# Ten staged batches in place of eleven in a sliding-window copy, and one split of the direct copies

## The chip, the core and the metric

The kernel runs on one core of one Trainium2 chip. The metric is device time in microseconds (us); lower is better. The time before is a median of three runs. The profile is of one execution. MB and GB/s are powers of ten; KB in the table of DMA issues are of 1024 bytes.

## The reference

Overlapping windows of 64 rows are copied out of a sequence, one every 32 rows. Nothing is computed; the output is the input written almost twice.

```python
def setup_inputs():
    batch, length, dim = (32, 4096, 256)
    window_size = 64
    stride = 32
    ...
def reference(x, window_size, stride):
    n_windows = (length - window_size) // stride + 1      # 127
    for i in range(n_windows):
        start = i * stride
        result[:, i] = x[:, start:start + window_size].copy()
```

In float32, x is 134.2 MB and the result 266.3 MB.

## The kernel before

A *block* is 32 rows of x, 32 KB. A batch has 128 blocks. Window w of a batch is blocks w and w + 1, so it is 64 KB, and a batch has 127 windows. Inner blocks stand in two windows each. The kernel only issues DMAs. It treats a batch in one of two ways.

*Staged batches* (`staged`, line 143) are 1, 4, 7, ..., 31: eleven of them. A staged batch is loaded once into a tile in SBUF, one block to each of the 128 partitions (4.19 MB), and stored twice from there, once as first halves of windows and once as second halves (8.39 MB). Its engine traffic is 12.58 MB. The stores write 128 half windows each, one more than the batch has, so a staged batch also writes wrong data into a half window of a neighbour. The neighbour's window there is written again later. The last batch, 31, is taken one block earlier so that nothing is written past the end of the output.

*Direct batches* (`direct`, line 146) are the other twenty-one. They are copied from DRAM to DRAM: windows overlap in the read and not in the write, so a window costs 64 KB read and 64 KB written, but passes the DMA engines once.

Three queues issue the work. All their transfers run on the core's same 16 DMA engines.

- ACT's queue (`ring_s`) carries the staged batches. `Staging.run` (line 116) works with six tiles: loads of the first six batches, their stores, loads of the other five, their stores. A load into a used tile waits until the tile's stores have landed (line 90); a store waits for its load (line 100). The first load is cut in four. The last batch's stores are cut as well (lines 103 to 106): the parts that matter for SP's last DMA come first, and five smaller ones (`end`) come last and are counted apart.
- SP's queue (`ring_d`) carries the direct batches: for each, 112 windows in seven *sixteens* of 16 windows (lines 161 to 164). They begin at window 15 where the batch before is staged, otherwise at window 0. Lines 170 to 187 keep an account, `share`, and with it send some sixteens as two *halves*, one DMA for the 16 first halves and one for the 16 second halves. In stretches which the account counts as loads three in four are halved, in others about one in seven (0.15), and all of them at the very start and around the turn to the second loads. Of 147 sixteens 55 are halved (110 DMAs), 92 are whole.
- POOL's queue (`ring_r`) carries the *edges* (line 166): the 15 windows of each direct batch that remain, which include those that a staged neighbour overwrites. POOL waits for `near` (line 192), which is the second last sixteen on SP; then each edge waits for the stores of its staged neighbours (lines 194 to 196). The last direct batch, 30, has its 15 windows in three parts: 4 windows, 9 windows cut into 16 columns (`columns`, line 200), and 2 windows that SP writes when the last staged batch's stores have landed (line 202).

[...]

A packet, in the profile's words, is one piece that a DMA engine moves for a queue. Pieces of loads and stores are cut at 16384 elements (`IN`, `OUT`), those of direct copies at 32768 (`DIRECT`); the packets that the page counts are 16 KB on ACT's queue and 32 KB on SP's. Each DMA adds on each engine it uses one small packet that reports its completion.

Of the kernel before, what the change touches and what calls it, by code (L numbers as in the profile page):

```python
# [125 lines left out]
@with_exitstack  # L126
def kernel(
    ctx: ExitStack,
    tc: tile.TileContext,
    x: bass.AP,  # L130
    window_size: bass.AP,
    stride: bass.AP,
    out: bass.AP,
):
    nc = tc.nc
    W, S = int(window_size), int(stride)
    B, L, D = x.shape
    n_win = (L - W) // S + 1
    assert out.shape == (B, n_win, W, D)
    c = Copier(x, out, B, L, D, W, S, n_win)  # L140


    staged = [*range(1, B, 3)]
    items = [(b, -1 if b == B - 1 else 0, c.nb) for b in staged]
    place = {b: g for g, (b, _, n) in enumerate(items) if n == c.nb}
    direct = [b for b in range(B) if b not in staged]
    pool = ctx.enter_context(tc.tile_pool(name="xb", bufs=1))
    st = Staging(c, tc, pool, x.dtype, items, 6)
    ring_d, ring_s, ring_r = nc.sync, nc.scalar, nc.gpsimd
    done = tc.alloc_semaphore("done")  # L150
    near = tc.alloc_semaphore("near")
    rest = tc.alloc_semaphore("rest")
    total = {done: 0, near: 0, rest: 0}

    def count(dma, sem):
        dma.then_inc(sem, 16)
        total[sem] += 16

    sixteens = []
    for b in direct:
        w = 15 if b - 1 in staged else 0
        sixteens += [(b, w + 16 * j) for j in range((c.nw - w) // 16)]
    singles = [(B - 1, c.nw - 1, 1)]
    edges = [(b, 0 if b - 1 in staged else 112, 15) for b in direct[:-1]]
    last = B - 2
    edges.append((last, 112, 4))

    first_loads, loads, stores = 6 * 17, 5 * 17, 6 * 34  # L170
    turns = share = 0
    with tc.tile_critical():  # L172
        st.run(ring_s)

        for i, (b, w) in enumerate(sixteens):
            sem = near if i == len(sixteens) - 2 else done
            second = turns - first_loads - stores
            loading = turns < first_loads or 0 <= second < loads
            share += 120 if turns < 16 or -8 <= second < 16 else 90 if loading else 18
            if share >= 120:  # L180
                share -= 120
                turns += 4
                count(c.windows(ring_d, b, w, 16, 0), done)
                count(c.windows(ring_d, b, w, 16, 1), sem)
            else:
                turns += 3
                count(c.windows(ring_d, b, w, 16), sem)
            if i == len(sixteens) // 2:
                for b, w, half in singles:
                    count(c.windows(ring_d, b, w, 1, half, 2048), done)  # L190

        ring_r.wait_ge(near, 16)
        for b, w, n in edges:
            for k in (b - 1, b + 1):
                if k in place and b != last:
                    st.wait_stored(ring_r, place[k])
            count(c.windows(ring_r, b, w, n), rest)


        count(c.columns(ring_r, last, 116, 9), rest)  # L200
        ring_r.drain()  # L201
        st.wait_stored(ring_d, place[B - 1])
        count(c.columns(ring_d, last, 125, 2), done)
        total[st.ended] = st.count[st.ended]
        for sem, n in total.items():
            ring_d.wait_ge(sem, n)
# [35 lines left out]
```

## Time and profile before

| | |
|---|---|
| median of 3 runs | 752.55 us (751.88 to 753.92) |
| span of the profiled execution | 742.1 us |
| median less that span | 10.45 us |
| busy time of POOL, the only engine with any | 12.7 us |
| bytes moved by the DMA engines, and mean rate | 313.26 MB, 422 GB/s |
| wait of SP for the last staged batch's stores (line 44) | 169.3 us, until its DMA at 723.77 us |

The profiled execution has no total of its own in the page beside its span; the median of the runs stands 10.45 us above the span.

The page's line of DMA rates shows forty slices of the span, 18.6 us each:

```profile
GB/s 361 424 430 427 435 431 428 423 435 425 428 427 426 428 428 420 429 435 427 427 427 412 433 435 431 427 436 432 434 424 429 430 424 426 428 435 432 421 420 253
```

Only the first and the last slice stand apart. The page's DMA issues show what the queues carry, with the median time from issue to landing in the last column:

```profile
out_dram<-in_x_dram SPq DMA_DIRECT2D x92, 1024.0 KB, 99.8
out_dram<-xb ACTq DMA_DIRECT2D x21, 4096.0 KB, 138.5
out_dram<-in_x_dram SPq DMA_DIRECT2D x110, 512.0 KB, 90.2
xb<-in_x_dram ACTq DMA_DIRECT2D x10, 4096.0 KB, 130.5
out_dram<-in_x_dram POOLq DMA_DIRECT2D x20, 960.0 KB, 37.9
```

A DMA lands some 100 us after its issue: the queues are filled far ahead of the engines. The chain of waits that ended last is of little use here, since 92% of it is put down to "another core or an unknown queue", which are the transfers themselves. So the case is read from the DMA tables, cut by time.

### The profile page before, as it was taken

Reading aid. Unit: us, or ns where it says so; the run is one execution under the profiler, and the core shown is the slowest. Engines: PE = TensorE matmul, PEld = TensorE weight load, DVE = VectorE, ACT = ScalarE, POOL = GpSimd, SP = SyncE. Lnnn points to the kernel's source line nnn. Section 1 sums busy time; section 2 is a strip of 40 time slices with the busy share of each in tenths; the row PEclk is TensorE's granted clock in tenths of the full one; section 3 lists DMA queues with packets and bytes.
Section 4 is the critical chain, followed back from the end, with each engine's and each line's share of the span. In section 5 each row is a group of like instructions: output and inputs, shape, how many; then the busy total and the mean of one; then the engine's idle time right before and its main releaser. Section 6 shows DMA issues by size and latency. Waiting matters only on the chain.

```text
span 742.1 us, 323 instructions
## 1 busy us (share of the span) xinstructions
POOL 12.7 (2%) x26
## 2 busy tenths in 40 slices
POOL 0000000000000000000000000000000000050100
DMA  8999999999999999999999999999999999999996
GB/s 361 424 430 427 435 431 428 423 435 425 428 427 426 428 428 420 429 435 427 427 427 412 433 435 431 427 436 432 434 424 429 430 424 426 428 435 432 421 420 253
DMA packets 18290, 313.26 MB, mean 422 GB/s; under 512 B 4336, under 2 KB 4336, under 8 KB 4528
## 3 DMA queue, kind: packets, MB, share of 16 engines
q1 hardware_dynamic: 8016, 154.32, 48.8%
q10 hardware_dynamic: 9104, 138.41, 44.0%
q0 software_dynamic: 1168, 20.51, 6.6%
q14 instruction: 2, 0.02, 0.0%
HBM read 220.95 MB, written 267.09 MB: 658 GB/s over the span
## 4 chain that ended last, share of the span: by engine, by line
another core or an unknown queue 92%; POOL 2%; issue 0%; POOLq 0%; SPq 0%
POOL out_dram L34 2%; POOLq L201 0%; POOLq L237 0%; SPq L172 0%; POOLq L114 0%
## 5 line engine op out<-in xcount | busy, mean ns | idle before, releaser
L34 POOL DMA_DIRECT2D out_dram<-in_x_dram x21 | 12.0, 575 | 685.4 <-DMA out_dram<-in_x_dram 648.7
L44 POOL DMA_DIRECT2D out_dram<-in_x_dram x1 | 0.6, 581 | 0.0
L223 POOL MEMSET const-float32-0.0<- 128x1 f32 x1 | 0.1, 98 | 0.2 <-issue 0.2
L223 POOL MEMSET const-bfloat16-1.0<- 128x1 bf16 x1 | 0.1, 101 | 0.0
L223 POOL MEMSET const-float32-1.0<- 128x1 f32 x1 | 0.1, 98 | 0.0
L223 POOL MEMSET const-uint8-127<- 128x1 uint8 x1 | 0.1, 98 | 0.0
## 6 DMA issues: line engine op xcount, KB each, us to landing
out_dram<-in_x_dram SPq DMA_DIRECT2D x92, 1024.0 KB, 99.8
out_dram<-xb ACTq DMA_DIRECT2D x21, 4096.0 KB, 138.5
out_dram<-in_x_dram SPq DMA_DIRECT2D x110, 512.0 KB, 90.2
xb<-in_x_dram ACTq DMA_DIRECT2D x10, 4096.0 KB, 130.5
out_dram<-in_x_dram POOLq DMA_DIRECT2D x20, 960.0 KB, 37.9
xb<-in_x_dram ACTq DMA_DIRECT2D x4, 1024.0 KB, 15.7
out_dram<-xb ACTq DMA_DIRECT2D x2, 1024.0 KB, 110.5
out_dram<-xb ACTq DMA_DIRECT2D x4, 512.0 KB, 94.4
```

The lines of the kernel that those rows point to most:

```text
L34: return q.dma_start(out=self.oap((b * self.nw + w0) * 2 + h, [[2 * blk, n], row]), in_=self.xap(b * self.nb + w0 + h, [[blk, n], row]), m ...
L44: return q.dma_start(out=self.oap((b * self.nw + w0) * 2, [[part, 16], [2 * self.blk, n], row]), in_=self.xap(b * self.nb + w0, [[part, 16 ...
L223: nc = _bacc.Bacc("TRN2", target_bir_lowering=False, num_devices=1)
```

## The change

Batch 25 leaves the staged list and becomes direct, so ten batches are staged: six and four. Twenty-two are direct. The account is gone, and no sixteen is halved: each direct batch is sent as 16, 16, 16, 32, 16 and 16 windows, at all times. `near` is still the second last piece. [...]

```diff
-    staged = [*range(1, B, 3)]
+    staged = [1, 4, 7, 10, 13, 16, 19, 22, 28, B - 1]
...
-    sixteens = []
+    pieces = []
     for b in direct:
         w = 15 if b - 1 in staged else 0
-        sixteens += [(b, w + 16 * j) for j in range((c.nw - w) // 16)]
+        for n in (16, 16, 16, 32, 16, 16):
+            pieces.append((b, w, n))
+            w += n
...
-    edges.append((last, 112, 4))
-
-    first_loads, loads, stores = 6 * 17, 5 * 17, 6 * 34
-    turns = share = 0
+    odd = -15 * len(edges) % 16
+    edges.append((last, 112, odd))
...
-        for i, (b, w) in enumerate(sixteens):
-            sem = near if i == len(sixteens) - 2 else done
-            second = turns - first_loads - stores
-            loading = turns < first_loads or 0 <= second < loads
-            share += 120 if turns < 16 or -8 <= second < 16 else 90 if loading else 18
-            if share >= 120:
-                share -= 120
-                turns += 4
-                count(c.windows(ring_d, b, w, 16, 0), done)
-                count(c.windows(ring_d, b, w, 16, 1), sem)
-            else:
-                turns += 3
-                count(c.windows(ring_d, b, w, 16), sem)
-            if i == len(sixteens) // 2:
+        for i, (b, w, n) in enumerate(pieces):
+            count(c.windows(ring_d, b, w, n), near if i == len(pieces) - 2 else done)
+            if i == len(pieces) // 2:
                 for b, w, half in singles:
                     count(c.windows(ring_d, b, w, 1, half, 2048), done)
...
-        count(c.columns(ring_r, last, 116, 9), rest)
+        count(c.columns(ring_r, last, 112 + odd, 13 - odd), rest)
```

## The prediction

> **What bounds the kernel now.** I read the page's share of busy time first. It shows no engine but POOL, at 12.7 us in all, so the span is made of transfers. The second view is the page's table of DMA queues:
>
> ```profile
> span 742.1 us, 323 instructions
> ...
> DMA packets 18290, 313.26 MB, mean 422 GB/s; under 512 B 4336, under 2 KB 4336, under 8 KB 4528
> ...
> q1 hardware_dynamic: 8016, 154.32, 48.8%
> q10 hardware_dynamic: 9104, 138.41, 44.0%
> q0 software_dynamic: 1168, 20.51, 6.6%
> ...
> HBM read 220.95 MB, written 267.09 MB: 658 GB/s over the span
> ```
>
> q1 is SP's queue (direct copies, DRAM to DRAM), q10 is ACT's (staged loads and stores), q0 is POOL's (edges). The shares add to 99.4% of 16 engines' span: the DMA engines are full, and a byte taken off them should shorten the span. One row stands against that at once: a direct byte is read and written in HBM, so it counts there twice and a staged byte once, and HBM already moves 658 GB/s.
>
> The third view was the DMA table cut into stretches, because the loads and stores of the staged batches alternate. From the byte counts, the first six loads end near 130 us, their stores near 405, the next five loads near 505, and the last stores at the end. Here are, one after the other, stretches 20 to 120 (loads), 140 to 400 (stores), 420 to 500 (loads) and 520 to 640 us (stores):
>
> ```profile
> DMA packets 2607, 42.86 MB, mean 429 GB/s; under 512 B 685, under 2 KB 685, under 8 KB 685
> q1 hardware_dynamic: 1299, 22.74, 53.1%
> ...
> DMA packets 6176, 111.19 MB, mean 428 GB/s; under 512 B 1312, under 2 KB 1312, under 8 KB 1328
> q1 hardware_dynamic: 3088, 63.48, 57.4%
> ...
> DMA packets 2109, 34.56 MB, mean 432 GB/s; under 512 B 560, under 2 KB 560, under 8 KB 560
> q1 hardware_dynamic: 1056, 18.35, 53.4%
> ...
> DMA packets 2838, 51.47 MB, mean 429 GB/s; under 512 B 597, under 2 KB 597, under 8 KB 597
> q1 hardware_dynamic: 1418, 29.53, 57.7%
> ```
>
> The rate is nearly the same in all four, 428 to 432. q1's part of the bytes is 53.1% in both load stretches (22.74 of 42.86; 18.35 of 34.56) and 57.1 to 57.4% in the store stretches. In the long store stretch both queues have 3088 packets: they take turns, packet by packet. The sizes follow: 16 KB on ACT's queue (138.41 MB over 9104 less one completion packet per DMA and engine), 32 KB on SP's. A full sixteen gives each engine three turns (two of 32 KB, one completion), a pair of halves four. With three quarters of the sixteens halved, that is 65.5/3.75 = 17.5 KB a turn against ACT's 16.4 x 16/17 = 15.4: 53.1%, the measured load stretch. With 15% halved, 65.5/3.15 = 20.8: 57.4%, the measured store stretch. So halves set only who gets how much of a full engine.
>
> The last view was the two ends (0 to 20 us, then 720 to 742), and the waits and timeline there:
>
> ```profile
> DMA packets 480, 7.34 MB, mean 367 GB/s; under 512 B 160, under 2 KB 160, under 8 KB 160
> ...
> DMA packets 619, 6.11 MB, mean 278 GB/s; under 512 B 213, under 2 KB 213, under 8 KB 389
> ```
> ```profile
> 649.11 10.25 POOL L34 DMA_DIRECT2D out_dram<-in_x_dram  x18 [648.67 <-DMA out_dram<-in_x_dram]
> 696.14 1.72 POOL L34 DMA_DIRECT2D out_dram<-in_x_dram  x3 [36.77 <-DMA out_dram<-xb]
> ```
>
> POOL begins its edges when SP's second last piece has landed (648.67), issues 18, and the next three wait until 696 for a store of staged data. Only the start and the last 22 us run below full rate.
>
> **The change, part by part.** The sum is made against the profiled span of 742.1 us. The median of the runs is 752.55; the 10.45 us between are taken as unchanged.
>
> *Batch 25 becomes direct.* ACT's queue loses one load and two stores of 4096 KB: 12.58 MB. SP's gains 112 windows of 64 KB, 7.34 MB, POOL's gains 16 rows of 64 KB less one in the columns, 0.98 MB. Engine bytes: 313.26 - 4.26 = 309.0 MB. HBM: a load of 4.19 MB goes, 8.32 MB of direct reads come, writes change by 0.07: 488.0 becomes 492.1 MB.
>
> *No halves, one 32 a batch.* A batch on SP is 14 packets of 32 KB and 6 completions: 20 turns. SP gets 14 x 32.77/20 = 22.9 KB a turn, ACT 15.4, so q1's part becomes 59.8% in loads and stores alike. HBM traffic per engine byte (1 plus q1's part) goes from 1.531 in loads and 1.573 in stores to 1.598. About 70 completions per engine go; in the stretches above the shares already reach 100%, with data alone, so I cost them at 0, with a gain of up to 0.7 us (0.1% of the span, the rounding of the shares). SP's issues are fewer too; they run some 100 us ahead of landing, so this is worth nothing while that lead is there.
>
> *The rate at 1.598.* No stretch of before holds it for long, so it is extrapolated: loads mean (429 + 432)/2 = 430.2 at 1.531, stores 428.2 at 1.573, a fall of 2.0 over 0.042; a further 0.025 takes 1.2 to 1.6. I take 426.6. Bounds: 432, the best stretch, and, for the load phases alone, 401, the mean from 3 to 20 us, where loads stand beside direct copies but the queues are only filling. In 122 to 132 us, where q1 had a 60% part beside loads, 433 was reached, but for 10 us only; I stay nearer to that.
>
> *The middle.* Before, 20 to 720 us moved 313.26 - 7.34 - 6.11 = 299.8 MB in 700 us, 428.3 GB/s. After, 295.5 MB at 426.6 takes 692.8 us: -7.2. With nothing lost in rate it would be 690.0, -10.0.
>
> *The tail* costs nothing if SP plus POOL and ACT still run out together. Turns per engine, from packets over 16: SP 501 less 3 for the last columns, then POOL 73, together 571; ACT 569. After: SP 22 x 20 + 2 = 442; POOL 73 + 2 + 1 - 1 = 75 (16 rows more, one DMA more, one column less), together 517; ACT 569 - 17 - 34 = 518. The balance stands. The waits in POOL's queue: SP ends near 161.5 MB/(0.598 x 426.6) = 633 plus 3 at the start, POOL starts near 638, and 19 edges without a late wait (18.7 MB at q0's 14.88 MB per 60 us in the stretch 660 to 720) feed it to about 713. The two edges beside batch 28 and the pieces queued behind them wait for its stores, which end some 47 us before ACT (8.39 MB at 10.67 MB per 60 us), near 687: the wait stays hidden by 26 us. With that cover gone, those four would run late, up to 4 MB at the end, about 9 us. ACT's second group is four loads; its first store waits for one of them with three queued behind, so its ring does not run dry. SP's last columns still wait for the last batch's stores, and lie beside five stores that SP does not wait for there. Tail and start: 0, bounds -1 to +3.
>
> Sum: 20 + 692.8 + 22 = 734.8 us of span, plus 10.45: **745.2 us**, 1.0% less. Bounds: 20 + 295.5/0.432 + 22 = 726 of span, so 736.5; and the worst load row, priced below.
>
> [...]
>
> **Rivals.**
> 1. *HBM reads become the bound in the load phases (slower).* In a load phase every engine byte is read from HBM, by both queues, and now 60% are also written. Loads of 41.9 MB at 40.2% of the bytes mean 104.3 MB pass in these phases: 244.5 us at 426.6. Against it: 429 and 432 in load stretches at 53%. For it: those stretches alone were held at 53%, and 3 to 20 us gave 401. At 401 the phases take 260.1 us, +15.6: 760.8. It decides from 104.3/(244.5 + 7.4 + 2.3) = 410 GB/s on: below that the result is over 0.3% slower.
> 2. *The same, milder: no change.* Load phases at 410 to 417 eat the gain: 750.3 to 754.8, middle 752.5. For it: the slices near 400 us, at the turn from stores to loads, are the weakest of the middle.
> 3. *The tail unbalances.* If POOL's last four pieces run late, +9 less what still overlaps, about +4: 749. For it: 0.69 busy in the last 22 us already. Against it: 517 against 518.
> 4. *The change does nothing to the rate* (the extrapolated loss does not come): 742.4, the forecast's lower side.
>
> **How the numbers follow.** About 0.3% (2.3 us) is what can be told from no change here. Forecast with rival 4: 0.56; rival 3: 0.06; rival 2: 0.15; rival 1: 0.23. So faster 0.62, same 0.15, slower 0.23. The forecast's own range is 740 to 750. The range of 8 in 10 runs from 740 to 758, which takes in rival 2 and the nearer half of rival 1.
>
> **What would show it.** Engine bytes 309.0 MB, HBM 492 MB, q1's part near 60% in load and store phases; packets per engine 445, 518 and 75; SP's second last landing near 632 us. Right, if the middle runs at 425 to 428 and the last 22 us stay near 6 MB. Wrong, if a load phase falls below 417 while stores keep 427 (rivals 1 and 2), or if one queue is alone for over 5 us at the end (rival 3).

## The result and the profile after

The changed kernel takes 761.23 us (median of 4 runs, 759.37 to 764.7) against 752.53 us of before (4 runs). The ratio is 1.0116, with a 95% interval of 1.0088 to 1.0145: slower by about 9 us, where 1% faster was forecast.

The page of the changed kernel, the lines that answer to those of before (queues: packets, MB, and the time of their packets as a share of 16 engines' time):

```profile
span 762.9 us, 251 instructions
...
DMA packets 16609, 308.99 MB, mean 405 GB/s; under 512 B 3184, under 2 KB 3184, under 8 KB 3360
...
q1 hardware_dynamic: 7120, 161.65, 51.5%
q10 hardware_dynamic: 8288, 125.83, 40.8%
q0 software_dynamic: 1200, 21.50, 6.8%
...
HBM read 225.08 MB, written 267.03 MB: 645 GB/s over the span
```

All that was counted came as counted: 308.99 MB, 492.1 MB in HBM, and 445, 518 and 75 packets on each engine (7120, 8288 and 1200 over 16). The engines are as busy as before, 99.1% against 99.4%, but move 405 GB/s in place of 422. So the same packets take longer: in the trace, a 32 KB packet takes 1227 ns in the mean in the stores of before (140 to 400 us) and 1271 in those of the changed kernel (160 to 420), a 16 KB packet 615 and 638; in the loads (20 to 120) 1219 became 1263, and 619 became 682. The DMA table cut by time, loads (20 to 120 us), stores (160 to 420) and loads (460 to 530):

```profile
DMA packets 2114, 40.18 MB, mean 402 GB/s; under 512 B 400, under 2 KB 400, under 8 KB 400
q1 hardware_dynamic: 1058, 24.18, 58.5%
...
DMA packets 5637, 107.34 MB, mean 413 GB/s; under 512 B 1024, under 2 KB 1024, under 8 KB 1040
q1 hardware_dynamic: 2818, 64.03, 59.8%
...
DMA packets 1469, 28.28 MB, mean 404 GB/s; under 512 B 263, under 2 KB 263, under 8 KB 263
q1 hardware_dynamic: 735, 17.04, 59.5%
```

q1's part of the bytes (24.18 of 40.18 MB, and so on; the last column is time) is 60% in loads and stores, as worked out, and both are slow: the loads by 6% against the 429 and 432 of before, the stores by 3.5% against 428. The start and the end are not where the time went. In the stretches of the span (length, POOL, clock, DMA share, GB/s) the middle alone is slow:

```profile
20.00:741.00 721.00, 12.95 (x23) 1.00 1.00 411
741.00:763.00 22.00, 0.00 (x0) 1.00 0.64 258
```

The last 22 us move 5.69 MB (258 GB/s), 0.4 MB less than before, which is 1 us. The timeline shows POOL's edges start at 663, with three late ones at 719 behind the stores, the same last three of the program as before:

```profile
663.10 7.93 POOL L34 DMA_DIRECT2D out_dram<-in_x_dram  x14 [662.66 <-DMA out_dram<-in_x_dram]
...
718.75 1.68 POOL L34 DMA_DIRECT2D out_dram<-in_x_dram  x3 [43.49 <-DMA out_dram<-xb]
```

### The profile page after: what moved, and what is told of

It reads as the page before. It is cut to its first block, busy times and chain, and to the rows that moved or that the text cites. A ratio compares the mean times of both kernels' runs of the same rounds, so it can differ in the third digit from the quotient of the medians.

```text
span 762.9 us, 251 instructions
## 1 busy us (share of the span) xinstructions
POOL 13.1 (2%) x27
## 2 busy tenths in 40 slices
DMA packets 16609, 308.99 MB, mean 405 GB/s; under 512 B 3184, under 2 KB 3184, under 8 KB 3360
## 3 DMA queue, kind: packets, MB, share of 16 engines
q1 hardware_dynamic: 7120, 161.65, 51.5%
q10 hardware_dynamic: 8288, 125.83, 40.8%
## 4 chain that ended last, share of the span: by engine, by line
another core or an unknown queue 93%; POOL 2%; issue 0%; POOLq 0%; SPq 0%
POOL out_dram L34 2%; POOLq L191 0%; POOLq L227 0%; SPq L173 0%; POOLq L114 0%
```

## The experiments

At first there were three theories for packets that take longer. *Theory 32*: the new pieces of 32 windows disturb the others. *Theory share*: the rate falls steeply with q1's part of the bytes. *Theory step*: the halved DMAs kept the sixteen engines in step, which the whole ones do not. A fourth possibility was batch 25 itself. The first four kernels cross ten and eleven staged batches with the ways to cut the direct copies.

**Ten staged, plain sixteens.**

```diff
-        for n in (16, 16, 16, 32, 16, 16):
+        for n in (16,) * 7:
...
-            ... near if i == len(pieces) - 2 else done)
+            ... near if i == len(pieces) - 8 else done)
```

> Ten staged, every direct piece a plain sixteen (no 32, no half); POOL's edges start six pieces earlier so that the queues still end together. q1's part of the bytes should be 58.6%. If the 32s disturb the engines (theory 32): the middle runs at 427 to 430 GB/s as before, time 742 to 747 us. If the rate falls steeply with q1's part beyond 57% (theory share): about 415 GB/s, 750 to 755 us. If the halves kept the sixteen engines in step (theory step): as slow as the changed kernel, 402 to 412 GB/s, 757 to 765 us.

Measured: 760.19 us, 1.0074 of before (1.0051 to 1.0097). Loads (20 to 120 us) and stores (140 to 400):

```profile
DMA packets 2205, 40.81 MB, mean 408 GB/s; under 512 B 447, under 2 KB 447, under 8 KB 447
q1 hardware_dynamic: 1100, 24.02, 57.1%
...
DMA packets 5864, 108.46 MB, mean 417 GB/s; under 512 B 1161, under 2 KB 1161, under 8 KB 1177
q1 hardware_dynamic: 2932, 63.31, 58.6%
```

At a part of 58.4 to 58.9% (24.02 of 40.81 MB, 63.31 of 108.46), with no 32 in the kernel, the rate is low: theory 32 falls.

**Eleven staged, cut as in the changed kernel.** The staged list of before in the changed kernel.

```diff
-    staged = [1, 4, 7, 10, 13, 16, 19, 22, 28, B - 1]
+    staged = [*range(1, B, 3)]
```

> Eleven staged as before, direct pieces as in the changed kernel (a 32, no halves), q1's part 59.8%. All three theories: the middle at 402 to 412 GB/s, as in the changed kernel, and with 4.26 MB more to move some 768 to 778 us (ACT alone for the end). If instead the tenth staged batch itself is the cause: 427 GB/s, below 757 us.

Measured: 770.33 us, 1.0214 (1.0174 to 1.0253). Loads (20 to 120 us) and stores (140 to 400):

```profile
DMA packets 2135, 40.62 MB, mean 406 GB/s; under 512 B 401, under 2 KB 401, under 8 KB 401
q1 hardware_dynamic: 1066, 24.41, 58.7%
...
DMA packets 5664, 107.80 MB, mean 415 GB/s; under 512 B 1023, under 2 KB 1023, under 8 KB 1039
q1 hardware_dynamic: 2832, 64.03, 59.6%
```

With batch 25 staged, the rate in loads and stores is as low as in the changed kernel: there it is the cut that makes it.

**Ten staged, with the account of halves of before.**

```diff
-    staged = [*range(1, B, 3)]
+    staged = [1, 4, 7, 10, 13, 16, 19, 22, 28, B - 1]
...
-    first_loads, loads, stores = 6 * 17, 5 * 17, 6 * 34
+    first_loads, loads, stores = 6 * 17, 4 * 17, 6 * 34
...
-            sem = near if i == len(sixteens) - 2 else done
+            sem = near if i == len(sixteens) - 25 else done
```

(The 4 and 9 windows of batch 30 are 5 and 8, as in the changed kernel.)

> Ten staged, with the account of halves of before, edges started where ACT has 75 turns left. All three theories: 427 to 432 GB/s in the middle, 742 to 747 us, faster than both kernels. If direct batch 25 in place of a staged one is itself the cause: 402 to 412 GB/s, over 757 us.

Measured: 760.47 us, 1.0072 (1.0049 to 1.0096). No theory had both: the halves bring the rate back in the loads (424 and 427 GB/s; the stores have 420), and the time, over 757 us, is the one that was put on batch 25 as the cause. So the time is lost without the new cut too, when batch 25 moves and the edges start earlier. The DMA table from 600 to 740 us shows where it is given back:

```profile
DMA packets 2835, 52.86 MB, mean 378 GB/s; under 512 B 801, under 2 KB 801, under 8 KB 801
...
q1 hardware_dynamic: 946, 19.53, 37.1%
q0 software_dynamic: 946, 19.53, 36.8%
q10 hardware_dynamic: 943, 13.80, 26.6%
```

The smaller part on SP leaves more of its work for the end, where it meets POOL's edges (here they wait for the 25th last sixteen): two queues of direct copies and one of stores, 74% of the bytes direct, and 378 GB/s. Counted in HBM that is 378 x 1.74 = 657 GB/s. The changed kernel's stores come to 412.8 x 1.597 = 659 and its loads to 402 x 1.602 = 644.

**Eleven staged, plain sixteens.** The kernel with eleven staged and 32s, with `(16,) * 7`.

> Eleven staged, all sixteens whole, q1's part 58.6%. Theory 32: 427 to 430 GB/s in the middle, some 752 to 756 us. Theory share: about 415 GB/s. Theory step: 402 to 412 GB/s, 768 us or more.

Measured: 766.84 us, 1.017 (1.0139 to 1.0201); 407 and 409 GB/s in loads, 417 in stores, as with ten. Here and in the other kernel with eleven staged batches and no halves, SP runs out early: from 700 to 742 us, 13.01 of 17.92 MB here are ACT's stores, at 427 GB/s but only 544 in HBM. Over the spans HBM moved 639 and 636 GB/s.

From these came *theory HBM*: the engines move the smaller of about 430 GB/s (the 428 to 432 of before) and what HBM allows, some 650 GB/s (the 644, 657 and 659 above) divided by 1 plus the direct part (the part of the engine bytes that are copied from DRAM to DRAM, by any queue). The next three tell it from theory step and from anything in turns or queues.

**Only direct copies, on two queues.**

```diff
-        st.run(ring_s)
...
+            q = ring_s if i % 2 else ring_d
-            count(c.windows(ring_d, b, w, n), near ...
+            count(c.windows(q, b, w, n), near ...
```

> Leaves out all staged batches (their windows are not written); the direct pieces of the changed kernel go alternately on SP's and ACT's queues, so every engine byte counts twice in HBM. Theory HBM (the engines move the smaller of about 430 GB/s and what HBM allows, some 650 GB/s over 1 plus the direct part): about 325 GB/s, a span near 575 us. Theory step or any theory of turns and queues alone: 405 to 430 GB/s, a span near 450 us.

Measured: 564.52 us in a single run. From its page:

```profile
span 562.7 us, 211 instructions
...
DMA packets 8321, 183.16 MB, mean 325 GB/s; under 512 B 2576, under 2 KB 2576, under 8 KB 2752
...
HBM read 183.14 MB, written 183.14 MB: 651 GB/s over the span
```

325 GB/s on the engines and 651 in HBM, as foretold; the span is 12 us below the 575 that went with it. From 20 to 400 us, a 32 KB packet takes 1585 ns in the mean.

**The same turns, without the HBM reads.** SP's pieces read a tile in SBUF.

```diff
+    def from_tile(self, q, t, b, w0, n):
+        blk = self.blk
+        return q.dma_start(
+            out=self.oap((b * self.nw + w0) * 2, [[blk, 2 * n], [1, blk]]),
+            in_=t[0 : 128 : 64 // n, :],
+            max_dma_last_dim=DIRECT,
+        )
...
-    st = Staging(c, tc, pool, x.dtype, items, 6)
+    st = Staging(c, tc, pool, x.dtype, items, 5)
+    spare = pool.tile([128, c.blk], x.dtype, name="spare")
...
+        c.load(ring_d, spare, 0, 0, (0, 1, 128, 1)).then_inc(filled, 16)
+        ring_d.wait_ge(filled, 16)
...
-            count(c.windows(ring_d, b, w, n), near ...
+            count(c.from_tile(ring_d, spare, b, w, n), near ...
```

> The changed kernel with SP's pieces read from a tile in SBUF in place of x (so the direct windows hold other data), and five staging tiles in place of six to make room; same packets, turns and q1's part of 60%, but an SP byte counts once in HBM. Theory HBM: 427 to 432 GB/s until POOL's edges begin. Theory step, theory 32 and theory share as a matter of turns: 402 to 413 GB/s as in the changed kernel.

Measured: 752.72 us in a single run. From 140 to 250 us:

```profile
DMA packets 2479, 47.60 MB, mean 433 GB/s; under 512 B 448, under 2 KB 448, under 8 KB 448
q1 hardware_dynamic: 1242, 28.64, 60.4%
q10 hardware_dynamic: 1237, 18.96, 40.2%
```

The same packets in the same turns, q1's part 60.2%, and 433 GB/s, with nearly every 32 KB packet at 1213 ns; from 140 to 640 us the mean is 428. (From 400 to 500 us, about when the second loads run, it has 424, and 1260 ns; why is open.) So the turns, the whole DMAs and the 32s are not what made the rate of 402 to 413. What cost was the read of x from HBM. Theory step falls, and theory share as a matter of turns. The whole time does not measure the gain: SP loads 4.2 MB more, and POOL's edges, which still read x, are most of what is left from 700 us on (305 GB/s to the end).

**Whole DMAs in place of halves, at the part of before.**

```diff
-            share += 120 if turns < 16 or -8 <= second < 16 else 90 if loading else 18
+            share += 60 if turns < 16 or -8 <= second < 16 else 45 if loading else 9
...
-                turns += 4
-                count(c.windows(ring_d, b, w, 16, 0), done)
-                count(c.windows(ring_d, b, w, 16, 1), sem)
+                turns += 5
+                count(c.windows(ring_d, b, w, 16, piece=16384), sem)
```

> Eleven staged as before; where a sixteen was halved, half as often a whole sixteen is sent in 16 KB packets (five turns in place of three), which gives the same 53.1% and 57.4% without one halved DMA. Theory HBM or share: 427 to 432 GB/s in loads and stores, within 0.5% of before. Theory step (halved DMAs keep the engines together): 402 to 417 GB/s, 765 us or more.

Measured: 753.87 us, 1.0001 (0.9987 to 1.0015). Loads (20 to 120 us) and stores (140 to 400):

```profile
DMA packets 2572, 42.14 MB, mean 421 GB/s; under 512 B 448, under 2 KB 448, under 8 KB 448
q1 hardware_dynamic: 1284, 22.61, 53.3%
...
DMA packets 6052, 109.34 MB, mean 421 GB/s; under 512 B 1147, under 2 KB 1147, under 8 KB 1163
q1 hardware_dynamic: 3026, 62.66, 57.5%
```

Not one DMA is halved and the time is that of before: halves matter only through the part that they give to SP. The rates, 421 to 426 GB/s, were below the 427 that was expected; so were those of before itself, next.

**Before, once more.** No edit.

> The kernel before, once more, for a second profile: the first 400 us of the kernel with ten staged batches and the account are the same program, and had 420 GB/s in the stores where before had 428. If that is a difference between executions or chips, this profile may show either; time within 0.3% of before.

Measured: 753.58 us, 0.9996 (0.998 to 1.0012), as it should be, and a profile that differs from the first one of the same kernel. From its page, then its loads (420 to 500 us) and stores (140 to 400) in the DMA table:

```profile
span 751.9 us, 323 instructions
...
DMA packets 18290, 313.26 MB, mean 417 GB/s; under 512 B 4336, under 2 KB 4336, under 8 KB 4528
...
HBM read 220.95 MB, written 267.09 MB: 649 GB/s over the span
```
```profile
DMA packets 2095, 34.33 MB, mean 429 GB/s; under 512 B 557, under 2 KB 557, under 8 KB 557
q1 hardware_dynamic: 1050, 18.25, 53.4%
...
DMA packets 6073, 109.32 MB, mean 420 GB/s; under 512 B 1293, under 2 KB 1293, under 8 KB 1309
q1 hardware_dynamic: 3039, 62.49, 57.5%
```

The span is 751.9, not 742.1, and the time of this profiled run is 753.67: span and time lie 1.8 us apart, as in the run of the changed kernel (762.9 and 764.7). So the first profile of before, whose own time is not on record, would be of an execution near 744 us, faster than any timed run of that kernel (751.7 to 756.7 us, on several chips). In the usual one the stores run at 420 GB/s, 661 in HBM. A 32 KB packet takes 1248 ns in the mean there, against 1227 in the first profile and 1213 in the run that reads from a tile: HBM already cost before some 3% in its stores.

**Half of the engines.** The kernel of direct copies alone, with `for n in (8,) * 14`, so that a DMA uses 8 engines.

> As the kernel of direct pieces alone (all staged batches left out), but in pieces of 8 windows, which use 8 of the 16 engines. If HBM as a whole sets the rate: 8 engines want about 8 x 27 = 216 GB/s, 432 in HBM, below its 650, so every 32 KB packet takes 1.21 to 1.23 us and some 215 GB/s are moved until POOL's edges. If a copy from DRAM to DRAM is slow for each engine by itself: half of the 328 GB/s of sixteen engines, about 164 GB/s.

Measured: 826.11 us in a single run. From 20 to 600 us:

```profile
DMA packets 5774, 125.49 MB, mean 216 GB/s; under 512 B 1928, under 2 KB 1928, under 8 KB 1944
...
q10 hardware_dynamic: 2877, 62.82, 25.2%
q1 hardware_dynamic: 2895, 62.66, 25.1%
```

216 GB/s with half of the engines busy is 27 for each, the same as 433 over sixteen, and a 32 KB packet takes 1214 ns. A copy from DRAM to DRAM is not slow for an engine. Sixteen of them at 27 GB/s would need 866 GB/s of HBM; they had 658 (329 GB/s on the engines from 20 to 400 us, 1585 ns a packet). Whether the bound is HBM itself or something on the way to it that the engines share, no run tells apart; "HBM" stands for both here.

**More staged, fewer direct.** If HBM holds before, 64 more blocks staged should help, until engine bytes bind.

```diff
+    part = 24
+    items.insert(10, (part, 16, 64))
...
-    first_loads, loads, stores = 6 * 17, 5 * 17, 6 * 34
+    first_loads, loads, stores = 6 * 17, 5 * 17 + 9, 6 * 34
...
-            share += ... else 90 if loading else 18
+            share += ... else 120 if loading else 50
```

(Batch 24 keeps its last two sixteens on SP, and three small DMAs fill the halves of windows that its staged blocks leave.)

> Before, with 64 blocks of batch 24 staged as a twelfth, half item (engine bytes 315.4 MB, HBM 485.9 MB) and more sixteens halved so that the queues still end together (loads 51.6% on SP, stores 55.4%). Theory HBM: loads 428 to 432 GB/s, stores 423 to 430, time 748 to 752 us, 0.2 to 0.7% faster than before; were only engine bytes to count, at before's rates, 757 to 759 us.

Measured: 753.66 us, 1.0005 (0.9994 to 1.0017): no change, between the two expectations. The stores rose to 424 GB/s, and the loads to 426 and 430, while the engine bytes rose by 2.1 MB, about 5 us at 424. The last 22 us moved 6.03 MB against 6.69 in the second profile of before, which is 1.6 us more. Gain and price cancel. That before lies near the crossing of the two limits would explain it, but no run shows the crossing itself; no kernel here beats before.

## Why the prediction was wrong

Rates below are engine GB/s, and HBM is that rate times 1 plus the direct part:

| stretch | direct part | rate | HBM |
|---|---|---|---|
| before, first profile: loads 20 to 120 | 53.1% | 429 | 656 |
| before, first profile: loads 420 to 500, stores | 53.1%, 57.1% | 432, 428 | 661, 672 |
| before again: loads 20 to 120 | 53.3% | 422 | 647 |
| before again: loads 420 to 500, stores | 53.2%, 57.2% | 429, 420 | 657, 661 |
| ten, plain sixteens: loads, stores | 58.9%, 58.4% | 408, 417 | 648, 661 |
| changed kernel: loads 20 to 120, stores | 60.2%, 59.7% | 402, 413 | 644, 659 |
| ten with halves, 600 to 740 us | 73.9% | 378 | 657 |
| only direct, 20 to 400 us | 100% | 329 | 658 |
| SP from a tile, 140 to 250 us | (60.2%) | 433 | 433 |

It is the sum of reads and writes that is steady, 644 to 672 GB/s in all rows but the last. In before's second profile the first loads read 422 GB/s and write 225, the stores read 240 and write 420; the direct copies alone read and write 329 each. No bound on reads or on writes alone fits all three.

- **The step that failed is the rate at 1.598.** It put 426.6 GB/s where the middle ran at (308.99 - 6.95 - 5.69) MB in 720.9 us, or 411.1, with the two ends as the page's stretches have them. The 295.5 MB take 718.8 us at that rate, 26.0 more than the 692.8 of the sum; another 2.1 us are 0.85 MB that the two ends moved less and left to the middle. Together that is the whole of 762.9 against 734.8. A line was drawn through two points (430.2 and 428.2) that lay near what the engines reached with a tile as SP's source (433 GB/s; 32 KB packets within some 1% of the 1213 ns there); beyond it the rate goes roughly with 650 over 1 plus the direct part, as the table's rows do, and that is steeper. The forecast asked 682 GB/s of HBM (1.598 x 426.6), where its own rows of 60 us and more show at most 675 (520 to 640 us); the 433 at a 60% part, to which it stayed nearer, stood in 10 us alone. Some 11 of the 26.0 us are not the change's: the 428.3 that the sum started from was that of a fast execution, and the second profile of before has 421.5 in the middle (299.24 MB in 709.9 us). From there the rate fell by 10.4, where a fall of 1.7 was forecast. A move of q1's part from 53 to 60% cost the loads 5 to 6% (429 to 404, 422 to 402 against the second profile of before).
- **"The engines are full, so a byte taken off them shortens the span" was the wrong reading.** An engine that waits for HBM counts as busy: it was 99.1% busy at 405 GB/s, and 99.8% at 329 in the kernel of direct copies alone (20 to 400 us). The share of busy time could not tell the two limits apart; bytes per busy time, set beside those of another mix, could.
- **The 10.45 us** between span and median were taken for something around the execution. Only 1.8 us are; the rest, if the first profile's run had the same 1.8, was that the profiled execution was a fast one, with stores at 672 GB/s of HBM that no later profile reached. In the sum, 8.65 of it were added that do not exist, and the changed kernel's profiled run was 3.5 us above its median: 745.2 + 28.1 - 8.65 - 3.5 = 761.2. That the median was missed by 16 us and not by 28 is therefore no merit of the sum. The gap also hid that usual runs lose time to HBM already.
- **Rival 1 had the right cause and too small a place.** It priced loads at 401 GB/s, and they ran at 402 and 404; but it kept 427 for the stores, which fell to 413, and put it down to reads in the load phases alone. Stores suffer too, at about 15 GB/s more of HBM traffic than loads (659 against 644). That its 401 came out is luck: it is the mean of 3 to 20 us at a 54% part, where both profiles of before have 401 and their loads after 20 us have 422 to 432; the changed kernel itself has 378 there. Rival 2's bounds, 410 and 417 GB/s, come to 750.8 and 755.1 us by its own sum, not 750.3 and 754.8.
- **What was right**: the bytes, the packets, the 59.8%, completions at next to no cost (the trace has them at 9 ns each, so the 72 fewer on each engine are worth 0.65 us, within the 0.7 that was allowed), and nearly the tail: three late edges stayed hidden, and the start and the end together cost the 2.1 us above.
- **What the runs show where the forecast needed 682.** Bytes that touch HBM once ran at 433 GB/s on the engines (SP from a tile, 140 to 250 us), copies from DRAM to DRAM at 329 (20 to 400 us). The first profile of before apart, the table's rows with direct copies put what HBM gives to one core here at 644 to 661 GB/s.

By HBM alone, the bytes over the 650 GB/s of theory HBM give, as an estimate, 757 us for the changed kernel's 492.1 MB, and 751 for before's 488.0. The spans were 762.9 and 751.9 in the profiles, and 758.8 and 757.2 in the other two kernels with ten staged. Some 6 us follow from the 4.1 MB alone. The rest of the changed kernel's span lies in its lower rates, most of all in loads (over the span HBM moved 645 GB/s against 649); no run takes these apart further.

## What to carry to other kernels

Count the traffic at both ends of a copy: a DRAM to DRAM byte uses HBM twice (direct copies alone: 183.16 MB on the engines, 366.28 in HBM), so work moved from staging to direct copies trades engine bytes for HBM bytes (here 4.3 MB less for 4.1 more), and both limits must be priced. Full busy shares and a flat rate do not say which limit holds (99.4% at 422 GB/s, 99.1% at 405); look for a stretch with another mix, or measure one, before a line is drawn beyond it. Where the trace gives the times of single packets, set their mean beside the shortest of the same size. Compare the profiled execution's span with several timed runs: a gap is a reason to doubt that the profile is a usual one.

## What was not expected of the hardware

Whether 53 or 100% of the bytes were direct copies, the table's rows of the later profiles have 644 to 661 GB/s in HBM, and eight engines that copied from DRAM to DRAM moved 27 GB/s each, as much as each of sixteen with a tile as SP's source. Loads beside direct copies got less than stores at the same part (408 against 417 GB/s, at 58.9 and 58.4%); why is open. So is why one profiled execution of before reached 672 GB/s in its stores: before's next profile and the kernel with the account and ten staged batches, whose first 400 us are the same program, both had 420 GB/s there, where it had 428. The later runs were made on three chips, with medians of before from 753.6 to 754.2 us; whether the chip or the execution made the first profile fast, the record does not say.
